# Early output of an MoE: gathers that add, one VectorE step in each expert's pause, other tiles and another order at the end

## The chip, the core and the metric

The kernel runs on one core of one Trainium2 chip. The metric is the device time of one execution in microseconds, lower is better. TensorE multiplies matrices, VectorE and ScalarE work on rows, GpSimd here issues the indirect DMAs and works on single columns, and SyncE issues the plain DMAs. Times in this text are microseconds (us), those inside a profile from the start of its span.

## The reference, cut to what matters

A trunk of two layers. Each ends with a mixture of experts, in which a token goes to 2 of 32 experts of one group; after the second layer every token's row is normalised and written out.

```python
def rmsnorm(x, g):
    xf = x.astype(jnp.float32)
    y = xf * lax.rsqrt(jnp.mean(xf * xf, axis=-1, keepdims=True) + RMS_EPS)
    return (y * g.astype(jnp.float32)).astype(x.dtype)
...
    def expert_block(args):
        e, xb = args
        return (jax.nn.silu(xb @ w_gate[e]) * (xb @ w_up[e])) @ w_down[e]
...
    for layer in range(DEPTH):
...
        h = h + hierarchical_moe(rmsnorm(h, ffn_norm[layer]), router_g[layer], router_g_bias[layer],
                                 router_e[layer], router_e_bias[layer], w_gate[layer], w_up[layer], w_down[layer])
...
    return rmsnorm(h, final_norm)[:, N_META:]
```

There are 1024 tokens and 16 rows of meta tokens that are dropped at the end; a row has 1024 float32 values, an expert's inner width is 256.

## The kernel before, in words

The change concerns the second layer's mixture, the last third of the program. `Moe.run` goes through 33 passes, e = 0 to 32. In pass e TensorE works on the gate and up products of expert e (96 rows at most) and on the down product of expert e−1. Float32 products are made from three pieces: ScalarE (L1552) and VectorE (L1553) split a weight tile `wp` in two roundings for a part of the products, the other part (`whole`, L953) runs in plain float32. SyncE loads weights (L898) into a ring of 17 slots of 1 MB; a load waits until VectorE has read the slot's old weights. GpSimd gathers an expert's rows (`ga`, L908) and scatters its results into the tensor `y_d` (L914), in which a token has two rows, one for each of its experts. VectorE writes an expert's results with its weights on them in L1002 (`rows`), once a pass.

In a pass VectorE's order is: down pieces, a pause in which it waits for ScalarE, up pieces, xq (L929), L1002, xT, hm (L978), and then the next pass's down pieces.

The class `Out` writes output while the loop still runs. On VectorE a chain of small steps (`order`: later, latest, masks, starts, places, suits) sorts the tokens by the later of their two experts. Eight indirect DMAs on GpSimd write the tokens' numbers to `list_d` (`place_ids`, L847), SyncE loads that list (`load_list`, L853), and VectorE makes row indices from it (`lists`, L858 to L862). The steps stand at the end of the pass (`end`), between hm and the next pass's pieces, except `sums`, which is at the pass's start.

The sorted tokens make seven tiles of 128. `EARLY_OUT` names for each tile the pass in whose beginning GpSimd gathers the tile's two rows of each token into two rooms (L1192). VectorE adds them (L1219) in the next pass, ScalarE squares and sums a row of 1024 (L1222), GpSimd makes the inverse root in 14 steps on single columns (`root`, L1228 to L1239 and L173), VectorE scales (L1242) and GpSimd stores by an indirect DMA (L1204). The tokens of the last three experts (`DIRECT`) are not in the tiles: their rows from these experts stay in SBUF, and only the other row is gathered (L1212). If a list does not suit (`bad`), the output is made again by `again` after the loop; that does not happen with these inputs.

The queues of the engines are in program order; a waiting instruction holds all that stands behind it on its engine. The order across engines is set by semaphores only.

## Time and profile before

| | us |
|---|---|
| median of three runs (1349.09 to 1350.46) | 1349.44 |
| profiled execution | 1349.53 |
| its span, first to last instruction | 1347.7 |
| TensorE busy in the span | 1267.6 (94%) |
| VectorE busy | 1055.0 (78%) |
| ScalarE busy | 748.0 (55%) |
| GpSimd busy | 401.9 (30%) |
| mean granted clock of TensorE | 0.971 |

The busy times are sums over the whole program, of which the part that is changed covers the stretch from about 1000 us to the end. What is limited by what has to be read from that stretch.

### The profile page before, as it was taken

How to read it: one execution, taken by the hardware profiler on the slowest of the kernel's cores; microseconds unless marked ns; L12 is line 12 of the kernel's file. 1: busy time of each engine (PE TensorE's matmuls, PEld its weight loads, DVE VectorE, ACT ScalarE, POOL GpSimd, SP SyncE). 2: the span in 40 equal slices, each digit the busy share in tenths (PEclk: the TensorE clock that was granted, in tenths of full speed). 3: DMA queues.
4: the chain of work that ended last, by engine and by line, in shares of the span. 5: the costliest groups of instructions: out<-in, count | busy, mean ns of one | idle time of the engine just before them, and what ended most of it. 6: DMA issues, size and time to landing. Idle time of an engine off the chain costs nothing. (4 is left out here: it accounts for less than half of the span.)

```text
span 1347.7 us, 22878 instructions
## 1 busy us (share of the span) xinstructions
PE 1267.6 (94%) x8029; PEld 1091.1 (81%) x8029; DVE 1055.0 (78%) x2490; ACT 748.0 (55%) x1595; POOL 401.9 (30%) x587
## 2 busy tenths in 40 slices
PE   7988999999999799999999999999699999999992
PEld 5977888888887799888998888999677778877771
DVE  5777888888888786667778677768879888888885
ACT  3435555555555555666655566555455566556552
POOL 0112122122220252022231222221312444545466
PEclk8998999999999899999999999999789999999996
DMA  8936999999980700304200010046779999999942
GB/s 306 409 125 203 369 363 370 349 352 358 358 304 30 267 25 1 120 1 170 93 25 16 9 36 17 17 161 224 279 259 293 340 389 377 366 369 357 342 175 77
DMA packets 81710, 293.12 MB, mean 217 GB/s; under 512 B 22897, under 2 KB 30321, under 8 KB 65075
## 3 DMA queue, kind: packets, MB, share of 16 engines
q1 hardware_dynamic: 63202, 245.54, 50.5%
q0 software_dynamic: 18384, 46.04, 9.9%
q8 instruction: 65, 1.06, 0.3%
q14 instruction: 59, 0.48, 0.1%
HBM read 270.75 MB, written 47.00 MB: 236 GB/s over the span
## 5 line engine op out<-in xcount | busy, mean ns | idle before, releaser
L1557 PE MATMUL gu<-wp,xT 128*96 128x256 f32 x512 | 147.3, 288 | 0.0
L1559 PE MATMUL gu<-wp,xT 128*96 128x256 f32 x512 | 143.4, 280 | 0.0
L1558 PE MATMUL gu<-wp,xT 128*96 128x256 f32 x512 | 143.3, 280 | 0.0
L1553 DVE TENSOR_TENSOR wp<-slotB,wp 128x512 fp32r<-128x512 f32 x160 | 107.0, 690 | 22.5 <-ACT wp L1552 21.6
L1557 PE MATMUL py<-wp,hT 128*96 128x512 f32 x256 | 112.7, 440 | 5.2 <-ACT hT L1552 5.2
L1552 ACT ACTIVATE wp<-slotB 128x512 fp32r<-128x512 f32 x160 | 96.0, 626 | 23.8 <-PE py L1559 20.2
L2460 POOL TENSOR_TENSOR hh<-hh,wt 128x512 f32<-128x512 f32 x56 | 72.4, 1293 | 111.4 <-ACT wt L2459 109.9
L1559 PE MATMUL py<-wp,hT 128*96 128x512 f32 x256 | 102.9, 402 | 2.1 <-DVE hT L1553 2.0
L914 POOL DMA_INDIRECT y_d<-xg,di x34 | 38.9, 1144 | 212.2 <-DVE xg L1002 205.7
L1558 PE MATMUL py<-wp,hT 128*96 128x512 f32 x256 | 101.5, 396 | 0.7 <-DVE wp L1553 0.7
L1552 ACT ACTIVATE xT<-xq 128x384 fp32r<-128x384 f32 x64 | 33.6, 526 | 111.1 <-DVE xq L929 107.9
L1557 PEld LDWEIGHTS gu<-wp,xT 128*96 128x96 f32 x512 | 84.8, 166 | 0.1
L1559 PEld LDWEIGHTS gu<-wp,xT 128*96 128x96 f32 x512 | 83.2, 162 | 0.0
L1558 PEld LDWEIGHTS gu<-wp,xT 128*96 128x96 f32 x512 | 82.9, 162 | 0.1
L953 PE MATMUL gu<-slotB,xq 128*96 128x256 f32 x320 | 75.6, 379 | 0.0
L2296 ACT ACTIVATE P<-bank,sm 128x400 f32<-128x400 f32 (+3 forms) x112 | 59.5, 539 | 25.8 <-DVE sm L2286 25.5
L2049 DVE TENSOR_TENSOR T<-bank,T 128x512 fp32r<-128x512 f32 (+2 forms) x112 | 53.7, 496 | 20.7 <-ACT T L2045 19.8
L929 DVE TENSOR_TENSOR xq<-pt,ffg 128x768 f32<-128x768 f32 (+1 forms) x66 | 61.0, 927 | 9.4 <-PE pt L926 9.4
L2463 DVE SCALAR_TENSOR_TENSOR hh<-bank,ri,hh 128x512 f32<-128x512 f32 x72 | 53.5, 747 | 16.8 <-PE bank L1559 16.4
L977 ACT ACTIVATE hm<-gu,table 96x256 f32<-96x256 f32 x64 | 30.0, 469 | 61.4 <-PE gu L1559 61.4
L1553 DVE TENSOR_TENSOR wp<-hh,wp 128x512 fp32r<-128x512 f32 x82 | 54.8, 689 | 11.8 <-ACT wp L1552 11.4
L2459 ACT ACTIVATE wt<-bank,ri 128x512 f32<-128x512 f32 x56 | 38.5, 688 | 41.7 <-PE bank L1559 34.6
(445 smaller groups left out, 4020.4 us busy)
## 6 DMA issues: line engine op xcount, KB each, us to landing
slotB<-w_up SPq DMA_DIRECT2D x20, 1024.0 KB
slotB<-w_down SPq DMA_DIRECT2D x20, 1024.0 KB
slotB<-w_gate SPq DMA_DIRECT2D x20, 1024.0 KB
hh<-w_gate SPq DMA_DIRECT2D x11, 1024.0 KB
hh<-w_up SPq DMA_DIRECT2D x10, 1024.0 KB
hh<-w_down SPq DMA_DIRECT2D x10, 1024.0 KB
slotR<-w_gate SPq DMA_DIRECT2D x10, 1024.0 KB
slotR<-w_up SPq DMA_DIRECT2D x10, 1024.0 KB
```

The costliest lines, as they stand in the source:

```text
L914: return nc.gpsimd.indirect_dma_start(out=self.r.y_d, out_offset=bass.IndirectOffsetOnAxis(ap=didx, axis=0), in_=y[:CAP], in_offset=None, ...
L929: nc.vector.tensor_tensor(x[:, 4 * a:4 * (a + w)].rearrange("p (a b) c -> p a b c", a=w), pt[:, a:a + w].rearrange("p a (b c) -> p a b c", ...
L953: nc.tensor.matmul(gu[:CAP, f * FE:f * FE + FE], lhsT=x[0][:, j], rhs=w[:, j], start=(f == 0 and j == 0), stop=False)
L1552: nc.scalar.activation(dH, src, AF.Copy)
L1553: nc.vector.tensor_tensor(dL, src, dH.bitcast(F32), op=OP.subtract)
L1557: nc.tensor.matmul(out, lhsT=aH, rhs=bH, start=start, stop=False)
L1558: nc.tensor.matmul(out, lhsT=aH, rhs=bL, start=False, stop=False)
L1559: nc.tensor.matmul(out, lhsT=aL, rhs=bH, start=False, stop=stop)
L2049: nc.vector.tensor_tensor(dL, src, dH.bitcast(F32), op=OP.subtract)
L2296: nc.scalar.activation(self.P[hd, qp][a][:, x0:x0 + xe], tt[:, :xe], AF.Exp, bias=sm[:, 3:4], scale=SCALE, accum_out=sm[:, x:x + 1])
L2460: done(end), s.op("G", end + s.LAT, 1170, lambda: nc.gpsimd.tensor_tensor(k.h[i][:, cs], k.h[i][:, cs], x, op=OP.add), lambda end: s.relea ...
L2463: s.op("V", now + s.LAT, 70 + 1.04 * 512, lambda: nc.vector.scalar_tensor_tensor(k.h[i][:, cs], p, self.ri[hd, i], k.h[i][:, cs], op0=OP.m ...
```

## The change

`EARLY_OUT` goes from (10, 14, 18, 22, 26, 30, 30) to (13, 17, 20, 24, 26, 29, 30). A tile's two gathers stand in two passes, and the second one adds to the first one's rows in the DMA (`compute_op`), so the VectorE addition of tiles is gone. ScalarE squares a tile in two halves into PSUM, and `root` has one step more, which adds the two sums. A tile goes through six passes: gather in pass f, adding gather in f+1, squares in f+2 (after the up pieces on ScalarE), root in f+3, scale in f+4, store in f+5; two rooms hold two tiles at a time. `end` and `middle` are replaced by `gap`, which puts at most a few VectorE instructions into the pause of a pass: the order's steps, cut into ten parts, in passes 1 to 15, and the scales. `place_ids` moves from pass 6 to 10, `load_list` from 8 to 11, `lists` from the end of pass 9 to the pause of pass 12. At the end tiles 5 and 6 use buffers of experts 27 and 26; the rows for the last three experts' tokens are gathered as before, one of them adding, and their roots, scales and stores come in another order.

```diff
-EARLY_OUT = (10, 14, 18, 22, 26, 30, 30)
+EARLY_OUT = (13, 17, 20, 24, 26, 29, 30)
...
-        return later, latest, masks, sums, starts, places, suits
+        return sums, {1: later, 2: latest, 3: masks, 4: numbers, 6: lambda: starts(0), 7: lambda: starts(3), 8: prefix, 9: places,
+                      11: suits, 12: self.lists, 15: self.tokens}
...
                 ps = self.down(hs, wd)
                 load(1)
+                if out:
+                    out.gap(e)
             if this and prev:
                 wp = self.up_pieces(e)
+                if out:
+                    out.squares(e)
...
-                    out.middle(e)
...
-            if out:
-                out.end(e)
+            if out and e == 0:
+                out.gap(0)
...
+    def fetch(self, x, rows, add=False):
+
+        n = rows.shape[0]
+        g = self.k.nc.gpsimd.indirect_dma_start(
+            out=x[:n], out_offset=None, in_=self.r.y_d, in_offset=bass.IndirectOffsetOnAxis(ap=rows, axis=0),
+            bounds_check=2 * L - 1, oob_is_err=False, compute_op=OP.add if add else OP.bypass)
+        self.got.append(g)
+        return g
...
+    def other(self, i, add=False):
+        self.fetch(self.sum[i], self.r.ti[:CAP, 1, i:i + 1], add)
...
+    def square(self, c, i, n=128):
         for j in range(2):
...
-        self.k.nc.scalar.activation(c[-1].bitcast(BF16)[:n, :D], c[0][:n], AF.Square, accum_out=self.st[:n, 0, i:i + 1])
+            self.k.nc.scalar.activation(self.junk[:n], c[:n, 512 * j:512 * j + 512], AF.Square,
+                                        accum_out=self.st[:n, 3 * j, i:i + 1])
 
...
+        eng.tensor_tensor(ss, ss, t, op=OP.add)
...
-        if e == 4:
-            sums()
+        if e == 0:
+            nc.vector.memset(self.st, 1.0)
+            nc.sync.dma_start(out=self.g, in_=bcast_row(k.A["final_norm"], D))
         if e == 6:
+            self.sums()
+        if e == 10:
             ids = []
             for i in range(len(r.tiles)):
                 x = r.place_ids(i)
                 self.apart(x, ids)
                 ids.append(x)
-        if e == 8:
+        if e == 11:
             r.load_list()
-        if 8 <= e < 8 + DIRECT:
-            r.load_tokens(e - 8)
-        for t, f in enumerate(EARLY_OUT[:-2]):
-            if e == f:
-                self.fetch(t, self.a)
+        if 12 <= e < 12 + DIRECT:
+            r.load_tokens(e - 12)
+        for t, f in enumerate(EARLY_OUT):
+            for j in range(2):
+                if e == f + j:
+                    x = self.fetch(self.rows[t], r.list[:, j, t:t + 1], j > 0)
+                    if t < len(EARLY_OUT) - 2:
+                        self.apart(x, [self.scat])
+            if e == f + 3 and t < 5:
+                self.root(t % 2)
+            if e == f + 5 and t < 5:
+                self.store_tile(t)
+        if e == NE - 1:
+            self.other(0, True)
+            self.other(1)
+            self.root(2)
+        if e == NE:
+            self.other(2)
+
+    def gap(self, e):
+
+        if e in self.order:
+            self.order[e]()
+        for t, f in enumerate(EARLY_OUT[:5]):
+            if e == f + 4:
+                self.scale(self.rows[t], t % 2)
+
+        if e == NE:
+            self.square(self.sum[0], 4, CAP)
+            self.root(3, n=2)
+
+    def squares(self, e):
+
+        for t, f in enumerate(EARLY_OUT[:5]):
             if e == f + 2:
-                self.root(0)
-            if e == f + 3:
-                self.store(t, self.a)
+                self.square(self.rows[t], t % 2)
         if e == NE - 2:
-            self.fetch(5, self.a)
-            self.fetch(6, self.b)
-            self.other(0, self.rows(0)[0])
+            self.square(self.rows[5], 2)
         if e == NE - 1:
-            self.root(0)
-            self.other(1, self.rows(1)[0])
-        if e == NE:
-            self.root(1)
-            self.other(2, self.rows(2)[0])
-            self.store(5, self.a)
-            self.root(2)
...
-        V = self.k.nc.vector
-        for f in EARLY_OUT[:-1]:
-            if e == f + 1 and f < NE - 2 or e == f == NE - 2:
-                self.add(V, self.a)
-            if e == f + 2 and f < NE - 2 or e - 1 == f == NE - 2:
-                self.scale(self.a, 0)
-        if e == NE - 1:
-            self.square(self.b, 1)
-
...
-        for x, f in ((0, later), (1, latest), (2, masks), (4, starts), (5, places), (7, suits), (9, r.lists), (11, r.tokens)):
-            if e == x:
-                f()
-        for f in EARLY_OUT[:-1]:
-            if e == f + 1 and f < NE - 2 or e == f == NE - 2:
-                self.square(self.a, 0)
-        if e == NE - 2:
-            self.add(V, self.b)
-        if e == NE - 1:
-            self.add(V, self.rows(0), CAP)
-            self.square(self.rows(0), 2, CAP)
...
+            self.square(self.rows[6], 3)
...
-        self.scale(self.b, 1)
+        self.scale(self.rows[5], 2)
+        self.store_tile(5)
...
-        self.scale(d[0], 2, CAP)
-        self.store(6, self.b)
+        for i in (1, 2):
+            self.add(self.sum[i], self.own[i], CAP)
+            self.square(self.sum[i], 4 + i, CAP)
+        self.scale(self.rows[6], 3)
         scatter()
-        self.root(3, V, 2)
-        self.scale(d[2], 4, CAP)
-        self.scale(d[1], 3, CAP)
-        for i in (0, 2, 1):
-            self.keep(d[i], r.ti[:CAP, 0, i:i + 1])
+        self.store_tile(6)
+        self.root(5, V, 2)
+        for i in (2, 0, 1):
+            self.scale(self.sum[i], 4 + i, CAP)
+            self.store(self.sum[i], r.ti[:CAP, 0, i:i + 1])
```

On VectorE, the place where the list's indices are made (`ids`, `list`; `wp` are weight pieces, `hm` and `hT` the expert's inner rows). Before:

```order
L978 SCALAR_TENSOR_TENSOR hm<-gu,table_5152,hm 96x256 [waits Activation_49]
L858 SCALAR_TENSOR_TENSOR ids<-past,ids 128x7 [waits DMASW5_49,DMASW6_49,DMASW4_49,DMASW7_49,DMASW3_49,DMAHW3_49,DMASW1_49,DMASW0_49]
L860 TENSOR_SCALAR ids<-ids 128x7 [waits DVE_49]
L862 TENSOR_SCALAR list<-ids 128x8 [waits DVE_49]
L862 TENSOR_SCALAR list<-ids 128x8
L1553 TENSOR_TENSOR wp_13239<-hh_11250,wp_13238 128x512 [waits DMAHW0_49,Activation_49]
L1553 TENSOR_TENSOR wp_13243<-hh_11250,wp_13242 128x512 [waits Activation_49]
L1553 TENSOR_TENSOR hT_13252<-ph,hT_13251 128x192 [waits Activation_49]
```

After, where the first two rows are the last down pieces of the pass and the wp rows behind L870 the up pieces:

```order
L1548 TENSOR_TENSOR wp_13469<-slotR_10855,wp_13468 128x512 [waits Activation_49]
L1548 TENSOR_TENSOR wp_13473<-slotR_10855,wp_13472 128x512 [waits Activation_49]
L866 SCALAR_TENSOR_TENSOR ids<-past,ids 128x7 [waits DMASW5_49,DMASW6_49,DMASW4_49,DMASW7_49,DMASW3_49,DMAHW4_49,DMASW1_49,DMASW0_49]
L868 TENSOR_SCALAR ids<-ids 128x7 [waits DVE_49]
L870 TENSOR_SCALAR list<-ids 128x8 [waits DVE_49]
L870 TENSOR_SCALAR list<-ids 128x8
L1548 TENSOR_TENSOR wp_13499<-slotR_10856,wp_13498 128x512 [waits DMAHW7_49,Activation_49]
L1548 TENSOR_TENSOR wp_13503<-slotR_10856,wp_13502 128x512 [waits Activation_49]
```

The same four instructions with the same wait for DMAs stand in another part of a pass, and three passes later.

On SyncE, the load of the list between weight loads. Before and after:

```order
L898 DMA qr<-w_gate 128x2048 [waits DMAHW2_49,DVE_49]
L853 DMA ids<-list_d 128x8x1 [waits DMASW5_49,DMASW4_49,DMASW6_49,DMASW3_49,DMASW7_49,DMASW2_49,DMAHW3_49,DMASW1_49,DMASW0_49]
L898 DMA qr<-w_up 128x2048 [waits DMAHW4_49,DVE_49]
```

```order
L906 DMA slot_11440<-w_gate 128x2048 [waits DMAHW3_49,DVE_49]
L861 DMA ids<-list_d 128x8x1 [waits DMASW5_49,DMASW4_49,DMASW6_49,DMASW3_49,DMASW7_49,DMASW2_49,DMAHW4_49,DMASW1_49,DMASW0_49]
L906 DMA slot_11441<-w_up 128x2048 [waits DMAHW5_49,DVE_49]
```

The load waits for all eight scatters; it has moved nine weight loads, three passes, down the queue.

On GpSimd, the last gathers of tiles (`list`) and of the last experts' tokens (`ti`), from the pass before the last two. Before:

```order
L1192 DMA out_11729<-y_d_5148,list 128x1024 [waits DMASW3_49,DMASW1_49]
L1192 DMA out_11730<-y_d_5148,list 128x1024
L1192 DMA xg_11723<-y_d_5148,list 128x1024 [waits DMASW5_49,DMASW6_49,DMASW2_49,PE_49]
L1192 DMA xgh<-y_d_5148,list 128x1024 [waits DMASW0_49,PE_49]
L1212 DMA hh_11725<-y_d_5148,ti 96x1024 [waits DMASW7_49,PE_49]
L914 DMA y_d_5148<-hh_11725,di_5154 2080x1024 [waits DVE_49]
L1228 TENSOR_SCALAR ost<-ost 128x1 [waits Activation_49]
L173 TENSOR_SCALAR ost<-ost 128x1 [waits Pool_49]
```

After:

```order
L1206 DMA xgh<-y_d_5148,list 128x1024 [waits DMASW7_49,PE_49]
L922 DMA y_d_5148<-hh_11725,di_5154 2080x1024 [waits DVE_49]
L1206 DMA xgh<-y_d_5148,list 128x1024 [waits DMASW3_49,DMASW2_49,DMASW1_49]
L1206 DMA xg_11723<-y_d_5148,list 128x1024 [waits DMASW5_49,DMASW4_49]
L922 DMA y_d_5148<-hh_11725,di_5154 2080x1024 [waits DVE_49]
L1214 DMA out<-out_11729,list 1024x1024 [waits DMASW6_49]
L1206 DMA xg_11723<-y_d_5148,list 128x1024 [waits DMASW5_49,DMASW4_49]
L1206 DMA hh_11725<-y_d_5148,ti 96x1024 [waits DMASW0_49,PE_49]
L1206 DMA hh_11725<-y_d_5148,ti 96x1024
```

Of the four gathers of tiles 5 and 6 that stood together, the second ones now wait for DMAs before them, and two gathers for the last experts stand in one group ahead of the root.

## Rows read from the trace of the kernel before

**Rows 1.** Busy time by stretch: us, then each engine, TensorE clock, DMA share, GB/s

```profile
1041.00:1065.00 24.00, 21.17 (x127) 16.63 (x126) 19.25 (x37) 11.73 (x22) 12.35 (x12) 1.00 0.99 336
...
1230.00:1272.00 42.00, 41.61 (x253) 33.66 (x252) 36.79 (x55) 24.77 (x46) 20.08 (x25) 1.00 1.00 360
...
1304.00:1326.00 22.00, 16.61 (x78) 11.48 (x76) 17.49 (x24) 11.65 (x23) 16.54 (x32) 0.86 0.20 63
```

**Rows 2.** VectorE timeline: start us, duration, line, output and inputs, idle before

```profile
999.67 1.27 DVE L1002 SCALAR_TENSOR_TENSOR xg<-py,table,xg 96x1024 f32<-96x1024 f32 x1
...
1052.55 1.27 DVE L1002 SCALAR_TENSOR_TENSOR hh<-py,table,hh 96x1024 f32<-96x1024 f32 x1
...
1065.11 1.27 DVE L1002 SCALAR_TENSOR_TENSOR xg<-py,table,xg 96x1024 f32<-96x1024 f32 x1
...
1075.23 1.27 DVE L1002 SCALAR_TENSOR_TENSOR xg<-py,table,xg 96x1024 f32<-96x1024 f32 x1
...
1085.32 1.27 DVE L1002 SCALAR_TENSOR_TENSOR xg<-py,table,xg 96x1024 f32<-96x1024 f32 x1
...
1087.37 0.48 DVE L978 SCALAR_TENSOR_TENSOR hm<-gu,table,hm 96x256 f32<-96x256 f32 x1 [0.32 <-issue]
1087.77 0.15 DVE L858 SCALAR_TENSOR_TENSOR ids<-past,ids 128x7 f32<-128x7 f32 x1
...
1101.94 1.37 DVE L1553 TENSOR_TENSOR wp<-slot,wp 128x512 fp32r<-128x512 f32 x2 [0.91 <-ACT wp L1552]
...
1105.50 1.27 DVE L1002 SCALAR_TENSOR_TENSOR hh<-py,table,hh 96x1024 f32<-96x1024 f32 x1
...
1303.61 1.27 DVE L1002 SCALAR_TENSOR_TENSOR hh<-py,table,hh 96x1024 f32<-96x1024 f32 x1
```

**Rows 3.** Costs by line on VectorE, 1000 to 1348 us: busy us, mean ns, idle before

```profile
L1242 DVE SCALAR_TENSOR_TENSOR out<-out,ost,out 128x1024 f32<-128x1024 f32 (+1 forms) x7 | 8.9, 1274 | 0.0
```

**Rows 4.** TensorE timeline: the first half of the next expert after the pause of 1101.94

```profile
1103.96 0.34 PE L1557 MATMUL gu<-wp,xT 128*96 128x256 f32 x1
```

**Rows 5.** ScalarE timeline after expert 5's rows: the wait for TensorE

```profile
1059.54 0.33 ACT L1552 ACTIVATE hT<-ph 128x192 fp32r<-128x192 f32 x1 [2.79 <-PE gu L953]
```

**Rows 6.** GpSimd timeline around the list's scatters

```profile
1046.57 1.24 POOL L847 DMA_INDIRECT list_d<-ids,place  x1 [1.57 <-DVE place L826]
...
1056.20 0.97 POOL L847 DMA_INDIRECT list_d<-ids,place  x1 [0.30 <-issue]
...
1089.44 1.05 POOL L869 DMA_INDIRECT token<-later_d,gi  x1 [0.30 <-issue]
```

**Rows 7.** SyncE's queue: the list's load and the next load

```profile
1064.99 0.38 SPq L853 DMA_DIRECT2D ids<-list_d  x1
1071.65 4.52 SPq L898 DMA_DIRECT2D qr<-w_up  x1
```

**Rows 8.** GpSimd timeline from the last gathers of tiles to the last store

```profile
1301.02 1.27 POOL L1192 DMA_INDIRECT xgh<-y_d,list  x1 [0.30 <-issue]
...
1307.80 0.19 POOL L1228 TENSOR_SCALAR ost<-ost 128x1 f32<-128x1 f32 x1 [0.49 <-ACT out L1222]
...
1315.28 0.19 POOL L1239 TENSOR_TENSOR ost<-ost 128x1 f32<-128x1 f32 x1
...
1325.17 1.58 POOL L1212 DMA_INDIRECT xgh<-y_d,ti  x1 [0.67 <-issue]
...
1340.65 0.91 POOL L1204 DMA_INDIRECT out<-out,ti  x1 [0.30 <-issue]
```

**Rows 9.** VectorE timeline of the same stretch: the additions that waited for gathers

```profile
1307.88 1.23 DVE L1219 TENSOR_TENSOR xg<-xg,xgh 128x1024 f32<-128x1024 f32 x1 [1.01 <-DMA xgh<-y_d,list]
...
1329.88 1.22 DVE L1219 TENSOR_TENSOR xgh<-xgh,xg 96x1024 f32<-96x1024 f32 x1 [0.94 <-DMA xgh<-y_d,ti]
```

**Rows 10.** GpSimd timeline: a tile's store and the gather that waits for it

```profile
1247.19 1.14 POOL L1204 DMA_INDIRECT out<-out,list  x1 [0.30 <-DVE wp L1553]
...
1259.61 1.08 POOL L1192 DMA_INDIRECT out<-y_d,list  x1 [3.60 <-DMA out<-out,list]
```

More of the change, by code (lines that the diff above doesn't have):

```diff
@@ L808, in sums, with starts @@
             k.nc.tensor.matmul(pr[:, 1], lhsT=k.ones, rhs=self.cnt, start=True, stop=True)
-        def starts():
-            a = tot
-            V.tensor_copy(tot, pr[:, 1])
-            for i, n2 in enumerate((1, 2, 4, 8, 16)):
+        def starts(i):
+            a = cum[(i - 1) % 2] if i else tot
+            if i == 0:
+                V.tensor_copy(tot, pr[:, 1])
+            for i, n2 in ((0, 1), (1, 2), (2, 4)) if i == 0 else ((3, 8), (4, 16)):
                 x = cum[i % 2]
@@ L1177, in __init__ @@
     def __init__(self, k, r, psum, out, room, g):
-        self.k, self.r, self.out, self.g = k, r, out, g
-        self.a, self.b = room, [k.xg[(NE - 6) % NX], k.xg[(NE - 5) % NX]]
-        self.st = k.route.tile([128, 4, 5], F32, name="ost")
+        self.k, self.r, self.out, self.g, self.a = k, r, out, g, room
+        x = [k.xg[e % NX] for e in range(NE)]
+        self.rows = [room[t % 2] for t in range(5)] + [x[NE - 5], x[NE - 6]]
+        self.own = x[NE - DIRECT:]
+        self.sum = [self.own[0], x[NE - 4], room[1]]
+        self.junk = psum.tile([128, 512], F32, name="junk", tag="junk", bufs=1)
+        self.st = k.route.tile([128, 4, 7], F32, name="ost")
         self.got, self.put = [], []
-        self.order = r.order(psum, room)
+        self.sums, self.order = r.order(self.junk, room)
     def apart(self, x, others):
@@ new lines, in store, with store_tile @@
+    def store(self, x, ids):
+        n = ids.shape[0]
+        p = self.k.nc.gpsimd.indirect_dma_start(
+            out=self.out[0], out_offset=bass.IndirectOffsetOnAxis(ap=ids, axis=0), in_=x[:n], in_offset=None,
+            bounds_check=S - 1, oob_is_err=False)
+        self.apart(p, self.put)
+        self.put.append(p)
+    def store_tile(self, t):
+        self.store(self.rows[t], self.r.list[:, 0, t:t + 1])
+    def other(self, i, add=False):
+        self.fetch(self.sum[i], self.r.ti[:CAP, 1, i:i + 1], add)
@@ L1241, in scale @@
     def scale(self, c, i, n=128):
-        self.k.nc.vector.scalar_tensor_tensor(c[0][:n], c[0][:n], self.st[:n, 2, i:i + 1], self.g[:n], op0=OP.mult, op1=OP.mult)
-    def rows(self, i):
-        x = self.k.xg
-        free = x[(NE - DIRECT) % NX]
-        return [(x[(NE - 4) % NX], self.a[1], self.b[1])[i], x[(NE - DIRECT + i) % NX], self.b[1] if i == 0 else free]
+        self.k.nc.vector.scalar_tensor_tensor(c[:n], c[:n], self.st[:n, 2, i:i + 1], self.g[:n], op0=OP.mult, op1=OP.mult)
     def begin(self, e):
         k, r, nc = self.k, self.r, self.k.nc
-        later, latest, masks, sums, starts, places, suits = self.order
-        if e == 4:
-            sums()
+        if e == 0:
+            nc.vector.memset(self.st, 1.0)
+            nc.sync.dma_start(out=self.g, in_=bcast_row(k.A["final_norm"], D))
         if e == 6:
+            self.sums()
+        if e == 10:
             ids = []
@@ L1343, in again @@
                     m.fetch(t, j, c[j])
-                self.add(nc.vector, c)
-                self.square(c, 0)
+                self.add(*c)
+                self.square(c[0], 0)
                 self.root(0, nc.vector)
-                self.scale(c, 0)
+                self.scale(c[0], 0)
                 nc.sync.dma_start(out=self.out[0, t * 128:(t + 1) * 128], in_=c[0])
```

52 lines of the change are left out of this document (10 added, 42 removed).

## The prediction

> **What bounds the kernel now.** I read the table of stretches first, then VectorE's timeline for the distance from one expert's rows (L1002) to the next, and last the queues of the three engines that issue DMAs. From 1041 us on, the loop of the second MoE keeps the 16 DMA engines busy all the time and TensorE and VectorE nearly so; after 1304 the DMA share falls to 0.20 and TensorE is busy in three quarters of the time [rows 1]. So there are two bounds: the loop's period, and after 1304 GpSimd's queue of gathers, roots and stores.
>
> I write A(e) for the start of L1002 in pass e, which stores expert e−1. An undisturbed period is 10.09 us, from 1075.23 to 1085.32 [rows 2]. Five periods from 999.67 to 1052.55 take 52.88, which is 2.43 over five such periods: the order steps at the end of passes 0 to 5. The next period takes 12.56, 2.47 over. The 22 periods from 1075.23 to 1303.61 take 228.38, 6.4 over: each of five tiles has an addition and a scale of 1.27 there [rows 3], and about half of the two shows. Those 11.3 us are all that the early output costs inside the loop.
>
> **What the change takes away.** In its pause before the up pieces VectorE waits 0.91 us for ScalarE, with 3.56 us to go to L1002 [rows 2]. A scale of 1.27 put there overshoots by 0.4, and the steps of the order, cut into more parts, by less than 0.7. Two rows take that up: VectorE idles 0.32 before hm at 1087.37 [rows 2], and TensorE starts the next expert's halves at 1103.96, 1.3 after the first up piece is made [rows 4]. So I cost these steps at nothing; without that cover the five scales would cost 2 us. The additions go to the gathers. That gives −2.4 for the order and −6.4 for the tiles. The long period after 1052.55 is unclear: ScalarE waited 2.79 us for TensorE at 1059.54 while GpSimd issued the eight scatters of the list [rows 5, 6]. These scatters return four passes later. The bounds are 0 and −2.5, nothing in the rows tells which, and I take −1.2.
>
> **What it adds in the loop.** *The list.* Eight scatters write it, SyncE loads it, and VectorE makes the indices. Before, the scatters ran from 1046.57 to 1056.20 (start of the last), the load was issued at 1064.99, and VectorE used it at 1087.77 with no wait shown: 22.8 us after the load's issue [rows 2, 6, 7]. Now the scatters stand in pass 10, the load at the start of pass 11 and the use in the pause of pass 12. GpSimd comes to the scatters where the small gather at 1089.44 stands, 4.1 after A [rows 2, 6], so the last starts at A(9)+4.1+9.6 = A(10)+3.6. It lands no later than 8.8 after its start (1056.20 to 1064.99, the load waits for it) [rows 6, 7]. I take 8, so the load leaves at A(11)+1.5. The use stands before the up pieces due 3.56 before A(12), that is at A(11)+6.5. How long the load takes no row shows. Below it is bounded by 6.9, the gather of 1301.02 awaited at 1307.88 when the DMA was nearly idle [rows 8, 9]; above by the 22.8. The nearest row is SyncE's own next load, which was issued at 1071.65 and held its queue for 4.52, to 1076.17: 11.2 after the list's load [rows 7]. I take 11.2. The indices are then there at A(11)+12.7, 6.2 late, plus 0.6 for the three steps, less 1.1 of slack (between the 0.32 and the 1.3 above, nearer the latter as TensorE sets the pace): **+5.7**. Behind the waiting step on VectorE stand the four up pieces, xq and L1002, so TensorE and ScalarE wait too. The bounds are +1.4 and +17. For its stand-still afterwards I add 1.0: between 1304 and 1326, with TensorE idle a quarter of the time, its granted clock was 0.86 of full speed on average [rows 1], so part of that stretch ran at the half level, 1.2 GHz.
>
> The Trainium skill, in "DMA: Bandwidth & Descriptors", section "Rules for kernel authors", says that a DMA with a non-contiguous last dimension becomes one descriptor an element; for this load that is 1024. By its section "Bandwidth" 64 packets an engine take about 0.67 us, and its section "Anatomy of one DMA" puts a fixed 2.0 us beside that: an estimate of 2.7, with no wait at all and a time about 6.7 us lower. That is the page's case for an idle DMA; the trace here has a share of 1.00, and the held queue of 4.52 us [rows 7] speaks against it.
>
> *The gathers.* A tile's second gather now adds to the first's rows, so it waits until these have landed, and ScalarE's squares come a pass later. While the DMA is full a transfer lands up to 12.4 us after its issue (the store of 1247.19, for which the gather of 1259.61 waited 3.60) [rows 10]; in the idle stretch it was 6.9. I take 10. For the first, second and fourth tile that leaves 1 to 4 us to spare. For the third (gathers in passes 20 and 21) and fifth (26 and 27), a root of up to 7.7 us stands on GpSimd ahead of the first or second gather [rows 8]. The rows then land about 2 us after they are due in ScalarE's queue, whose next work is xT: **+2 each**, bounds 0 and 3.3. Whether an adding gather moves more bytes no row shows; at 360 GB/s [rows 1] one more read of 0.5 MB would be 1.4 us a tile on engines whose share has fallen to 0.20 by 1304, so nothing.
>
> **The end.** Set 0 at 1303.61 (A(30)). Now the last store is issued at 1340.65, 37.0 after it, and the span ends 7.05 later, at 44.1 [rows 2, 8]. After, GpSimd has in this order: the first gather of tile 6 (done at 1.3), the scatter of expert 29 (2.8), a store (4.1), the adding gather, which waits for that scatter to land (4.7 as from 1325.17 to 1329.88 [rows 8, 9]; done 8.4), two gathers for the last experts (11.4), a root of 15 steps for tile 5 (12.9 to 19.4; the 14 steps of before took 7.7 [rows 8], other ones 5.1 to 5.5), the scatter of expert 30 (20.4), its landing and the last gather (26.7), a root for two columns at once (32.0). VectorE then scales tile 6 (33.4), makes its own root (35.8) and three scales; the last store is issued at 39.8 and the span ends at 46.8: **+2.7**. Tile 5's squares wait for a gather that leaves only in their own pass, so TensorE stands some 5.5 us in pass 30; that makes its last rows come at 27, still ahead of GpSimd's 32.0, and costs nothing more. Removing one root and one store at the end is paid for by three waits for landings in a row.
>
> **The sum.** 1347.7 − 2.4 − 6.4 − 1.2 + 5.7 + 1.0 + 2 + 2 + 2.7 = 1351.1. The profiled execution took 1349.53, 1.83 more than its span and 0.09 more than the median of 1349.44. So: **1352.9 us**, 0.26% above the median. About 0.2% (2.7 us) is what a measurement here tells from no change.
>
> **The rivals.**
> *The list lands in time.* Then 6.7 us fall away: 1346.2. It decides if the load lands within 6 us of its issue; for it speaks that the use had no wait before, against it that this use was 22.8 us behind, and now is 5. Chance 0.30. The Trainium skill's estimate above is this case.
> *The DMA sets the loop's pace.* Its share is 0.99 to 1.00 from 1041 to 1272 [rows 1]. If weights were late, a shorter loop would only wait for them: the 10.0 us of gain are lost, the list's stall costs nothing as the loads catch up, and the tail's 2.7 stays: 1352.2. Against it: the pause of 1101.94 ended with ScalarE, not with a load [rows 2], and after 1304 the share is 0.20. Chance 0.10.
> *The steps don't fit the pauses.* The scales and the order's steps push every up piece back, so that half of the 8.8 us is not gained, and the eight scatters stall TensorE as before: 1352.9 + 4.4 + 1.2 = 1358.5. Chance 0.15.
> *The forecast*: the list is late by 3 to 10 us. Chance 0.45.
>
> The bounds together: the list at +1.4 without a drop of the clock, gathers in time and the scatters harmless give 1342.3; the list at +10 and the late gathers at 3.3 each give 1360. I take **1343 to 1360**; the list at +17 lies outside. Faster by over 0.2% (under 1346.7): 0.29, nearly all from the first rival. Within 0.2%: 0.26, from the low part of the forecast and the second rival. Slower: 0.45.
>
> **What would show it.** In pass 12 VectorE's first index step should wait some 6 us on a DMA, with TensorE idle behind it; the periods of passes 1 to 6 and of tiles 1, 2 and 4 should be 10.1; ScalarE's squares of tiles 3 and 5 should wait for gathers; the last third should be GpSimd's chain, its last store about 40 us after expert 29's rows. The prediction is wrong if the list step shows no wait, or if GpSimd's chain ends before TensorE's last rows.

## The result

| | before | after |
|---|---|---|
| median of ten runs each | 1349.27 | 1356.07 |
| lowest to highest | 1347.88 to 1352.24 | 1353.15 to 1361.27 |
| profiled execution | 1349.53 | 1353.48 |
| its span | 1347.7 | 1351.7 |
| mean granted clock of TensorE | 0.971 | 0.963 |

The ratio is 1.0051, with an interval of 1.0034 to 1.0068: slower by half a per cent, 6.8 us where 3.5 were forecast. The profiled execution is one of the lower ones of after; its rows explain 4.0 us, and what makes up the other 2.6 of the median no row shows.

The table of stretches of after, which answers to [rows 1]:

```profile
1105.00:1147.00 42.00, 35.97 (x204) 29.69 (x203) 29.65 (x53) 20.42 (x38) 15.49 (x13) 0.92 0.99 348
...
1230.00:1272.00 42.00, 41.49 (x253) 34.20 (x252) 35.60 (x54) 25.82 (x50) 20.24 (x27) 1.00 1.00 349
...
1304.00:1326.00 22.00, 16.11 (x92) 12.55 (x90) 13.27 (x21) 11.84 (x27) 14.04 (x23) 0.92 0.53 124
1326.00:1351.70 25.70, 2.66 (x11) 1.54 (x10) 12.99 (x23) 4.59 (x13) 13.59 (x23) 0.61 0.29 94
```

A stretch with 6 us of idle TensorE has appeared at 1105. From 1230 to 1272 the DMA is as full as before and moves 349 GB/s instead of 360. From 1304 to 1326 its share is 0.53 instead of 0.20; the adding gathers of tiles 5 and 6 run there now, issued at 1303.59 and 1313.87, where before issued its last gather of a tile at 1301.02 [rows 8].

VectorE's timeline of after: the rows of an expert (L1010, which was L1002), and the first index step of the list. It answers to [rows 2]:

```profile
997.76 1.27 DVE L1010 SCALAR_TENSOR_TENSOR xg<-py,table,xg 96x1024 f32<-96x1024 f32 x1
...
1048.35 1.27 DVE L1010 SCALAR_TENSOR_TENSOR hh<-py,table,hh 96x1024 f32<-96x1024 f32 x1
...
1088.70 1.27 DVE L1010 SCALAR_TENSOR_TENSOR xgh<-py,table,xgh 96x1024 f32<-96x1024 f32 x1
1101.97 1.27 DVE L1010 SCALAR_TENSOR_TENSOR hh<-py,table,hh 96x1024 f32<-96x1024 f32 x1
...
1114.76 0.17 DVE L866 SCALAR_TENSOR_TENSOR ids<-past,ids 128x7 f32<-128x7 f32 x1 [7.97 <-DMA ids<-list_d]
...
1118.59 1.27 DVE L1010 SCALAR_TENSOR_TENSOR hh<-py,table,hh 96x1024 f32<-96x1024 f32 x1
1129.25 1.27 DVE L1010 SCALAR_TENSOR_TENSOR xg<-py,table,xg 96x1024 f32<-96x1024 f32 x1
...
1220.06 1.27 DVE L1010 SCALAR_TENSOR_TENSOR xgh<-py,table,xgh 96x1024 f32<-96x1024 f32 x1
1234.22 1.27 DVE L1010 SCALAR_TENSOR_TENSOR hh<-py,table,hh 96x1024 f32<-96x1024 f32 x1
...
1306.47 1.27 DVE L1010 SCALAR_TENSOR_TENSOR hh<-py,table,hh 96x1024 f32<-96x1024 f32 x1
1321.99 1.27 DVE L1010 SCALAR_TENSOR_TENSOR xg<-py,table,xg 96x1024 f32<-96x1024 f32 x1
```

The first five periods take 50.59 us, 10.12 each: the order's steps are hidden. Four periods are over 12 us: 13.27 to 1101.97, 16.62 to 1118.59, 14.16 to 1234.22, and 15.52 to 1321.99. In all A(1) to A(30) takes 308.71 us, 16.1 over 29 periods of 10.09, where before took 303.94, 11.3 over. A(1) itself stands 1.9 earlier than in [rows 2]; over the profiles of this study it lies between 994.9 and 999.7, so lengths from A(1) on are what can be compared. From A(1) to the end after takes 5.9 us more than before, not 4.0. The wait of 7.97 for the list explains the second; TensorE stands behind it:

```profile
1116.06 0.53 PE L1553 MATMUL gu<-wp,xT 128*96 128x256 f32 x1 [6.03 <-DVE wp L1548]
```

ScalarE's timeline of after has the waits in the other three:

```profile
1095.02 0.33 ACT L1547 ACTIVATE hT<-ph 128x192 fp32r<-128x192 f32 x1 [2.86 <-PE gu L961]
...
1222.47 0.60 ACT L1231 ACTIVATE junk<-out 128x512 f32<-128x512 f32 x1 [3.92 <-DMA out<-y_d,list]
...
1311.16 0.60 ACT L1231 ACTIVATE junk<-xgh 128x512 f32<-128x512 f32 x1 [6.20 <-DMA xgh<-y_d,list]
```

The first is the wait of [rows 5] again, now in the pass to which the eight list scatters have moved. The second is the third tile (gathers in passes 20 and 21), the third is tile 5 counted from 0 (gathers in passes 29 and 30). Here "the third tile" counts from 1 and "tile 5" from 0, as in the prediction. The issuers' queues of after, GpSimd's first, then SyncE's; they answer to [rows 6 to 8, 10]:

```profile
1092.90 0.97 POOL L855 DMA_INDIRECT list_d<-ids,place  x1 [0.30 <-issue]
...
1103.52 2.60 POOL L922 DMA_INDIRECT y_d<-hh,di  x1 [7.12 <-DMA y_d<-xgh,di]
...
1201.05 1.13 POOL L1206 DMA_INDIRECT out<-y_d,list  x1 [0.52 <-issue]
...
1210.51 1.62 POOL L1206 DMA_INDIRECT out<-y_d,list  x1 [5.75 <-DMA out<-y_d,list]
...
1303.59 1.69 POOL L1206 DMA_INDIRECT xgh<-y_d,list  x1 [4.07 <-issue]
...
1313.87 1.60 POOL L1206 DMA_INDIRECT xg<-y_d,list  x1 [3.60 <-DMA y_d<-hh,di]
...
1329.46 1.01 POOL L1206 DMA_INDIRECT out<-y_d,ti  x1 [2.70 <-DMA y_d<-xg,di]
...
1344.65 0.91 POOL L1214 DMA_INDIRECT out<-hh,ti  x1 [0.30 <-issue]
```

```profile
1100.43 0.38 SPq L861 DMA_DIRECT2D ids<-list_d  x1
1100.90 5.23 SPq L906 DMA_DIRECT2D slot<-w_up  x1
```

The list's load is used 14.3 us after its issue and holds SyncE's next load for 5.23. The third tile's adding gather leaves at 1210.51, because GpSimd waited for the first gather, and has landed at 1222.47, 12.0 later. The last store is issued at 1344.65, 38.2 after A(30).

The queues' page of after, and the same row of before (packets, MB, share of 16 engines' span):

```profile
q0 software_dynamic: 18384, 46.04, 10.8%
...
HBM read 270.75 MB, written 47.00 MB: 235 GB/s over the span
```

```profile
q0 software_dynamic: 18384, 46.04, 9.9%
```

GpSimd's transfers have the same packets and bytes and take more of the engines' time: 0.108 of 1351.7 is 146.0 us of all 16, against 133.4. The share is printed to 0.1%, so each of these is good to some 0.7 us.

### The profile page after: what moved, and what is told of

It reads as the page before. It is cut to its first block, busy times and chain, and to the rows that moved or that the text cites. A ratio compares the mean times of both kernels' runs of the same rounds, so it can differ in the third digit from the quotient of the medians.

```text
span 1351.7 us, 22865 instructions
## 1 busy us (share of the span) xinstructions
PE 1267.8 (94%) x8029; PEld 1100.0 (81%) x8029; DVE 1045.9 (77%) x2483; ACT 749.7 (55%) x1615; POOL 391.0 (29%) x580
## 3 DMA queue, kind: packets, MB, share of 16 engines
q1 hardware_dynamic: 63202, 245.54, 50.4%
q0 software_dynamic: 18384, 46.04, 10.8%
## 5 line engine op out<-in xcount | busy, mean ns | idle before, releaser
L922 POOL DMA_INDIRECT y_d<-xg,di x34 | 34.2, 1006 | 202.6 <-DVE xg L1010 194.9
L2276 DVE TENSOR_REDUCE mx<-bank 128x1 f32<-128x400 f32 (+3 forms) x112 | 55.5, 505 | 7.6 <-PE bank L2262 5.6
```

What stands on the lines that cost most here:

```text
L2276: V.tensor_reduce(m[:, ci:ci + 1], t[:, :e], axis=AX.X, op=OP.max)
```

## Experiments

Theory 1 at the start: the list's late load is what costs. Rivals: the time lost there would be lost elsewhere, as the DMA or GpSimd's queue is the bound; or the adding gathers cost DMA time, which the prediction had at nothing. A(e) is as before, now with L1010. Each kernel is compared with runs of before on the same chip.

**1. The list a pass later** (before's median 1348.02 there, also for 2 to 4)

```diff
-EARLY_OUT = (13, 17, 20, 24, 26, 29, 30)
+EARLY_OUT = (14, 17, 20, 24, 26, 29, 30)
...
-                      11: suits, 12: self.lists, 15: self.tokens}
+                      11: suits, 13: self.lists, 15: self.tokens}
```

> The changed kernel with the list's index steps in the pause of pass 13 in place of 12, and the first tile gathered in pass 14 in place of 13. My theory: the list lands about 14 us after its load is issued, so a use ten microseconds later finds it there; VectorE's wait of 8.0 us on the list vanishes, the period of 16.62 becomes 10.1, and the time falls by 6 to 7 us, to about 1349.5. Rival: the list step only shows a backlog of the DMA that some later transfer would show anyway (weights late, first tile late), so the wait turns up elsewhere and the time falls by less than 2 us.

Measured: 1354.48, ratio 1.0047 (1.0022 to 1.0071), not told apart from after's 1.0051: a fall of under 2 us, as the rival had it. In the profiled execution the use still waited:

```profile
1121.01 0.17 DVE L866 SCALAR_TENSOR_TENSOR ids<-past,ids 128x7 f32<-128x7 f32 x1 [4.65 <-DMA ids<-list_d]
```

The load, issued at 1103.06, was used 18.0 us later, so a pass more of room did not cover it in this execution: the load took 3.7 us longer than in after, and the stall behind the list's scatters, which in after held the use back by 3.2 us as well, did not come. What was won was not kept: period 30 (to A(31)) was 19.24 instead of 15.52.

**2. Gathers ahead of roots**: in addition, GpSimd issues a pass's gathers ahead of its root.

```diff
         for t, f in enumerate(EARLY_OUT):
             for j in range(2):
...
+        for t, f in enumerate(EARLY_OUT):
             if e == f + 3 and t < 5:
                 self.root(t % 2)
```

> As the run before, and in each pass's beginning GpSimd issues the gathers of tiles ahead of the roots. Theory: the third tile's rows were late because a root of 7 us stood ahead of its first gather; now the gather leaves 7 us earlier, ScalarE's wait of 3.9 us for them and the long period of 14.16 vanish, that of 10.83 for the fifth tile too: 4 to 5 us less than the run before. Rival: the adding gather itself is slow (a transfer that reads its destination), and the rows are late by 2 us or more in any order.

Measured: 1355.89, one run, so 4 to 5 us less did not show. It speaks most against theory 1. The list was in time, the third tile's period was 10.09, the scatters did not stall, and the rows of expert 24 stood at 1241.07, 10.8 us ahead of before's 1251.88 (0.8 of it at A(1)). None of it was left at the end (span 1354.1). TensorE's timeline:

```profile
1255.39 1.94 PE L961 MATMUL gu<-hh,xq 128*96 128x256 f32 x8 [1.46 <-DMA hh<-w_gate]
...
1259.38 1.97 PE L961 MATMUL gu<-slot,xq 128*96 128x256 f32 x8 [1.88 <-DMA slot<-w_up]
...
1271.52 1.97 PE L961 MATMUL gu<-slotR,xq 128*96 128x256 f32 x8 [1.53 <-DMA slotR<-w_up]
...
1284.26 2.97 PE L961 MATMUL gu<-slotR,xq 128*96 128x256 f32 x8 [2.41 <-DMA slotR<-w_up]
```

TensorE waits for weights, for which it waits nowhere from 1235 to 1300 in before and after. The periods to A(26) to A(29) are 11.35, 13.88, 12.15 and 14.39: 11.4 us over. Then ScalarE waits 10.98 for tile 5, and the period to A(31) is 20.50. The loop without the list's wait runs into the DMA here. The table of stretches of this kernel has the rate:

```profile
1225.00:1250.00 25.00, 24.00 (x141) 19.46 (x140) 20.72 (x32) 14.28 (x27) 10.40 (x9) 1.00 1.00 336
1250.00:1275.00 25.00, 20.05 (x122) 16.20 (x121) 17.59 (x27) 12.22 (x26) 11.69 (x21) 1.00 0.99 344
```

**3. Tile 5's squares and root a pass later**, on top of 2:

```diff
         if e == NE - 1:
             self.other(0, True)
             self.other(1)
-            self.root(2)
...
+        if e == NE - 1:
+            self.square(self.rows[5], 2)
+            self.root(2)
...
-        if e == NE - 2:
-            self.square(self.rows[5], 2)
```

> As the run before, and the squares of tile 5 stand on ScalarE in the pause of pass 31 in place of pass 30, with the root for them behind them. Theory: TensorE's stall of 5.4 us in pass 30 vanishes (period of 15.52 to about 10.5), but the end is set by GpSimd's chain of gathers, roots and scatters, so the end moves by less than 1.5 us. Rival: TensorE's last rows set the end, and the time falls by the whole stall, 4 to 5 us.

Measured: 1359.59, ratio 1.0089 (1.007 to 1.0108): slower than after, which neither expectation had. The stall of pass 30 went into two, with periods of 13.98 and 13.91; ScalarE's timeline:

```profile
1313.42 0.60 ACT L1231 ACTIVATE junk<-xgh 128x512 f32<-128x512 f32 x1 [4.73 <-DMA xgh<-y_d,list]
...
1324.07 0.60 ACT L1231 ACTIVATE junk<-xg 128x512 f32<-128x512 f32 x1 [7.10 <-DMA xg<-y_d,list]
```

**4. The list loaded twice**: after, with a second load of the same shape ahead of the real one.

```diff
         if e == 11:
+            with nc.allow_non_contiguous_dma("one number a row"):
+                nc.sync.dma_start(out=self.twice, in_=r.list_d.rearrange("(t p) o -> p (t o)", p=128))
             r.load_list()
```

> The changed kernel with a second load of the same list, into a tile that nobody reads, ahead of the first on SyncE's queue. Theory: the list's 1024 single elements take their time one after another, so a second such load ahead of it makes VectorE's wait on the list longer by 6 to 12 us (from 8.0 to 14 to 20). Rival: the wait is the latency behind the queued weights, which a small load more does not change: the wait stays at 7 to 10 us.

Measured: 1355.52. VectorE waited 4.8 us longer than in after, and SyncE's queue was held by the real load too:

```profile
1114.33 0.17 DVE L866 SCALAR_TENSOR_TENSOR ids<-past,ids 128x7 f32<-128x7 f32 x1 [12.78 <-DMA ids<-list_d]
```

```profile
1099.56 8.39 SPq L861 DMA_DIRECT2D ids<-list_d  x1
1108.05 5.07 SPq L906 DMA_DIRECT2D slot<-w_up  x1
```

One such load costs some 5 to 8 us on this queue. The increase of 4.8 lies between the two expectations, nearer the theory's. The one run's 1355.52 lies among after's, but A(1) came 2.8 us earlier and the scatters did not stall, which gave 3.1 back; from A(1) to the end this profile is 4.8 us longer than after's, so in this execution the longer wait did reach the end. The trace also shows what such a load is made of: the hardware queue has 64242 packets instead of 63202, 1040 more for the second load of 1024 numbers.

**5 and 6. Plain second gathers**: the second gather overwrites instead of adding, in experiment 2's kernel and in after itself (before's median 1349.33, also for 7 and 8).

```diff
-            bounds_check=2 * L - 1, oob_is_err=False, compute_op=OP.add if add else OP.bypass)
+            bounds_check=2 * L - 1, oob_is_err=False, compute_op=OP.bypass)
```

> The kernel of gathers_ahead_of_roots, with every adding gather as a plain one to the same place: as many gathers, bytes and waits, but the second row replaces the first, so the sum of the two rows is left out. In gathers_ahead_of_roots the loop was 10.8 us ahead of the kernel before by expert 24, and lost it when TensorE waited for up and gate weights in passes 25 to 28, with the DMA engines full at 335 to 344 GB/s against 360 before. Theory: the adding gathers make the DMA engines read the destination too, 0.5 MB a tile and some 10 us in all, and this makes the weights late. Then the rate at a full share goes back to about 360, the last weights land 7 to 10 us earlier, the waits for weights go, and the time falls by 6 us or more, below that of the kernel before (about 1343). Rival: the weights are late because the loop runs ahead of the DMA, whatever the gathers do: the waits stay and the time changes by less than 2 us.

> The changed kernel itself, with every adding gather as a plain one to the same place (the sum of the two rows is left out). The first theory: about 4 to 6 us less than the changed kernel, since the third tile's rows come earlier and the last weights too, but the wait of 8 us on the list stays, so about 1350. Rival: nothing, as in the changed kernel the loop is not ahead of the weights.

Measured: 1352.27 for experiment 2's kernel, ratio 1.0019 (1.0004 to 1.0033), where it was 1355.89; and **1349.58 for after**, ratio 0.9996 (0.9976 to 1.0015), where it was 1356.07. The intervals of after with and without the adding (1.0034 to 1.0068) do not meet: the adding in the DMA costs about 6.5 us by the medians, nearly all of the loss (before's medians beside them are 1349.33 and 1349.27). That is as the theory had it for after; in experiment 2's kernel the fall is 3.6 us against one run, not the 6 or more that the theory had. VectorE's timeline of after with plain gathers, and its queue row:

```profile
1119.50 0.17 DVE L866 SCALAR_TENSOR_TENSOR ids<-past,ids 128x7 f32<-128x7 f32 x1 [9.51 <-DMA ids<-list_d]
...
1225.66 1.27 DVE L1010 SCALAR_TENSOR_TENSOR xgh<-py,table,xgh 96x1024 f32<-96x1024 f32 x1
1236.50 1.27 DVE L1010 SCALAR_TENSOR_TENSOR hh<-py,table,hh 96x1024 f32<-96x1024 f32 x1
...
1307.96 1.27 DVE L1010 SCALAR_TENSOR_TENSOR hh<-py,table,hh 96x1024 f32<-96x1024 f32 x1
1321.36 1.27 DVE L1010 SCALAR_TENSOR_TENSOR xg<-py,table,xg 96x1024 f32<-96x1024 f32 x1
```

```profile
q0 software_dynamic: 18384, 46.04, 10.2%
```

The list's wait is even longer (9.51). The third tile's period fell from 14.16 to 10.84 and that of pass 30 from 15.52 to 13.40, 5.4 us together, and these are the places where a gather is waited for. The two profiled executions differ by only 1.1 us, since this one is the third longest of its ten: A(1) stands 2.0 later in it and the list's two periods are 3.7 longer, and all the rest is 6.7 shorter. GpSimd's transfers take 0.102 of 1350.6 us, 8.2 less than in after; over the study the queue's share is 10.7% to 11.0% in the six profiles with adding gathers and 9.9% to 10.2% in the eight without. From 1304 to 1326 both move 124 GB/s, at a DMA share of 0.39 here and 0.53 in after. In experiment 2's kernel the waits for weights are gone; from 1250 to 1275 the DMA moves 361 GB/s instead of 344:

```profile
1250.00:1275.00 25.00, 24.30 (x150) 20.07 (x149) 20.10 (x31) 15.73 (x30) 10.92 (x21) 1.00 0.99 361
```

What it gains is lost again at the end: GpSimd's first gather for tile 5 waited 8.32 for a scatter to land (1289.25), the root behind it came late for VectorE's scale (a wait of 4.44, period 14.54), and ScalarE waited 12.16 for tile 5's second gather:

```profile
1306.77 0.60 ACT L1231 ACTIVATE junk<-xgh 128x512 f32<-128x512 f32 x1 [12.16 <-DMA xgh<-y_d,list]
```

**7. The order's steps in the pauses alone**: before with this one part, the scatters in pass 8, the load in pass 9, the indices and the first tile's gathers in the pause of pass 11.

```diff
-EARLY_OUT = (10, 14, 18, 22, 26, 30, 30)
+EARLY_OUT = (11, 14, 18, 22, 26, 30, 30)
...
+                if out:
+                    out.gap(e)
...
-        if e == 6:
+        if e == 8:
...
-        if e == 8:
+        if e == 9:
             r.load_list()
...
+    def gap(self, e):
+        if e in self.order:
+            self.order[e]()
+        if e == EARLY_OUT[0]:
+            self.fetch(0, self.a)
```

> The kernel before with only the order's steps moved into VectorE's pauses (passes 1 to 13); tiles, roots and the end as before. The scatters of the list stand in pass 8, its load at the start of pass 9, the index steps in the pause of pass 11, and the first tile's gathers right behind them; the other tiles stand where they did. Theory: 2.4 us of order steps go, nothing is added, the weights have enough lead for that: a period of 10.1 in passes 1 to 6 and 1346 to 1347. Rival: the loop already runs at the DMA's pace, and what it gains early is lost to weights before the end: no change within 1 us.

Measured: 1355.55, ratio 1.0044 (1.0031 to 1.0058), more than either expectation. The part itself did what it should: A(1) to A(8) took 70.82 instead of 75.56; 2.5 of this is the scatters' stall, which came a period later here (14.00), and 2.3 the order's steps. But I had left three passes between the first two tiles, which share their rooms, and GpSimd's gather waited for the first tile's store:

```profile
1141.46 1.02 POOL L1202 DMA_INDIRECT out<-y_d,list  x1 [10.72 <-DMA out<-out,list]
```

VectorE's addition then waited 7.49, and that period was 20.72. The experiment shows what a tight schedule costs while the DMA is full, and does not price the part.

**8. Before again**, one more profile of the old kernel:

> The kernel before, once more. ScalarE's wait of 2.8 us for TensorE while the eight scatters are issued (period of 12.56) was there in the changed kernel (13.28), but not in the three kernels run since with the same scatters (10.16). Theory: it is an event that comes in some executions and not in others, and has no fixed place: this run may show it elsewhere or not at all. Rival: it belongs to the scatters in pass 6 and comes again, at 2 to 3 us.

Measured: 1352.91. The period that holds the eight scatters, 12.56 in [rows 2], was 15.00 here, and ScalarE waited longer:

```profile
1060.34 0.33 ACT L1552 ACTIVATE hT<-ph 128x192 fp32r<-128x192 f32 x1 [3.56 <-remote]
```

In the profiles of this study the pass of the scatters took 12.6 to 15.0 in six (the two of before, after, 5, 6 and 7) and 10.0 to 10.2 in seven (1 to 4, 9, 11 and 12), among these 12, in which nothing around the scatters differs from before. The stall has moved with the scatters, to passes 10 (after, 5, 6) and 8 (7), so it belongs to them, and it is not there every time; what decides it stays open. It goes by sets of runs: all four of 5 to 8, which ran on one chip at one time, had it, and none of 1 to 4, of 9 and 10 or of 11 and 12.

**9. Pauses without adding gathers**: before with the order's steps and the additions in the pauses, a tile's two plain gathers a pass apart, in two rooms a tile (before's median 1348.67, also for 10).

```diff
-            if e == f:
-                self.fetch(t, self.a)
-            if e == f + 2:
-                self.root(0)
+            if e == f and t:
+                self.fetch(t, self.pair(t), (0,))
+            if e == f + 1:
+                self.fetch(t, self.pair(t), (1,))
+            if e == f + 3:
+                self.root(0)
...
+    def gap(self, e):
+        if e in self.order:
+            self.order[e]()
...
+            if e == f + 2:
+                self.add(self.k.nc.vector, self.pair(t))
```

> A version built from the kernel before: the order's steps in VectorE's pauses, and the tiles with two plain gathers a pass apart, where the next tile's first rows go to the room that the last tile's addition has freed; the addition (1.21 us) in the pause two passes after the first gather, squares behind the up pieces, root a pass later, the scale where the kernel before has it (0.4 us shows), the store at the end of that pass. Tiles 5 and 6 as in the kernel before, in the other order. Theory: what costs the change its gain is the read that the adding gathers add to full DMA engines, the wait for the list and the chain at the end; without all three about 1.5 us of order steps and 4.5 of tiles stay gained, the weights' lead is enough, and the time is 1343 to 1345. Rival: any lead of the loop over the DMA is lost again to late weights: 1348 to 1350.

Measured: 1360.74, ratio 1.0089 (1.0067 to 1.0111), far above both expectations. VectorE's additions waited for the second gather, issued a pass earlier; the waits from 1100 to 1320, with their sum, number and longest:

```profile
DVE out L1232 <- DMA out<-y_d,list: 17.7, 4, 6.2
```

A pass is too short for a gather here, and on VectorE everything stands behind the addition. So a version without adding gathers and without late rows has not been measured.

**10. The list's scatters in two halves**: before, with four in pass 6 and four in pass 7.

```diff
-        if e == 6:
-            ids = []
-            for i in range(len(r.tiles)):
+        if e in (6, 7):
+            ids = self.ids = self.ids if e == 7 else []
+            n = len(r.tiles)
+            for i in range(n // 2 * (e - 6), n // 2 * (e - 5)):
```

> The kernel before with four of the list's eight scatters in pass 6 and four in pass 7. In six of ten profiles so far the period behind the eight scatters was 2.5 to 5 us long, in four it was not. Theory: eight scatters hold GpSimd's queue and the DMA for 10 us; four of them do no harm, and both periods are 10.1 to 10.5. Rival: the event has nothing to do with their number: a period of 12 us or more in one of the two passes.

Measured: 1348.75, one run. Both periods were 10.1; as 9, run beside it with all eight scatters in one pass, had no stall either, this does not tell whether four scatters do less harm than eight. A(30) stood 3.1 us earlier than in [rows 2], at 1300.49. The next period gave it back, 13.92 instead of 10.89, as VectorE waited for tile 5:

```profile
1306.22 1.23 DVE L1219 TENSOR_TENSOR xg<-xg,xgh 128x1024 f32<-128x1024 f32 x1 [2.48 <-DMA xgh<-y_d,list]
```

**11 and 12. Fewer weights**: the loads of the down weights of experts 20 to 31 are left out, 12 MB, in experiment 2's kernel and in before (before's median 1349.35).

```diff
+        if self.out and e >= 20 and m == 2:
+            return
```

> The kernel of gathers_ahead_of_roots (the change with the list a pass later and the gathers ahead of the roots, adding gathers as they are) without the loads of the down weights of experts 20 to 31, 12 MB or some 33 us of full DMA engines; the products then use what the slots held before, so the output of these experts is left out. Theory: with room on the DMA engines the weights are no longer late, the loop keeps the 10.8 us by which it was ahead of the kernel before at expert 24, and the gathers at the end land in 5 to 7 us: 1344 to 1347, 9 to 12 us less than with all weights (1355.9). Rival: the end is GpSimd's own chain, whatever the DMA does: 1352 or more.

> The kernel before, without the same loads (the output of experts 20 to 31 is left out as well). Theory: its loop does not wait for weights and its gathers hardly for room, so it gains 1 to 3 us: 1346 to 1348. Rival: it too is bound by the DMA at the end, and gains 5 us or more.

Measured: 1350.83, ratio 1.0019 (1.0001 to 1.0036), for experiment 2's kernel, 5 us less than that kernel's one run with all weights and nearer to the rival's 1352 than to the theory's 1344 to 1347; and 1349.59, ratio 0.9994 (0.9978 to 1.001), for before, which gains nothing. So before loses no time to its weights, and experiment 2's kernel does. With fewer weights its periods from A(24) to A(30) are all 10.1 and the DMA share from 1275 to 1300 is 0.30, and still ScalarE waits for tile 5; ScalarE's row, and GpSimd's issue of that gather:

```profile
1302.57 0.60 ACT L1233 ACTIVATE junk<-xgh 128x512 f32<-128x512 f32 x1 [7.75 <-DMA xgh<-y_d,list]
```

```profile
1296.22 1.63 POOL L1208 DMA_INDIRECT xgh<-y_d,list  x1 [3.45 <-issue]
```

The gather lands 6.4 us after its issue even here, and is issued too late. From A(1) to A(30) this loop is 3.9 us shorter than before's (300.04; 7.0 are lost in one period, at the third tile), and its tail from A(30) is 48.2 instead of 44.1: the late gather of tile 5 and the chain of GpSimd behind it give all of it back. This profile is the second shortest of its ten, 4.2 us below their median; against before's span its 3.2 us are the 3.4 by which A(1) came earlier. No kernel here beat before by more than the measurement tells.

## Why the prediction was right, and where it was not

The forecast, slower by some microseconds and inside the range, was right. The profiled execution even met the sum: 1351.7 for 1351.1. That is luck: the loop lost 4.1 us more than the terms say, the tail lost 1.6 less, and A(1), ahead of everything that the sum is about, came 1.9 earlier. And the loss in the medians has another cause than the sum names. The steps:

- **The order's steps, −2.4**: right. The first five periods are 0.1 over five times 10.09, where 2.43 had been. So the third rival, that the steps don't fit the pauses, fell, though the stall at the scatters that it also had did come.
- **The tiles' additions and scales, −6.4**: right. The periods of the first and second tile are 10.1. That of the fourth, which was to be so too with 1 to 4 us to spare, is 10.83, as its squares waited 2.27 for the adding gather.
- **The list's scatters, −1.2**: wrong. The stall moved with the scatters and was 3.2 where before had 2.5, so +0.7. It belongs to the scatters (8) and comes in some executions.
- **The list, +5.7 and +1.0**: the mechanism was right, the size by luck. The step waited 7.97 with TensorE idle behind it, and its two periods are 7.1 over. But the load landed after 14.3 us instead of 11.2, and the lateness came out as forecast because the stall at the scatters put the use 3.2 later. The Trainium skill ("DMA: Bandwidth & Descriptors", "Rules for kernel authors") says that such a load becomes one descriptor an element; the trace agrees, with 1040 packets for one more load of 1024 numbers (4). The estimate of 2.7 us that I made from its sections "Bandwidth" and "Anatomy of one DMA", whose figures stand there for DMAs that GpSimd issues, did not hold for this load of SyncE on a full DMA (14.3), and so the rival by it fell.
- **Late gathers, +2 each**: the third tile cost 4.1, the fifth 0.9 and the fourth, which had none in the sum, 0.7. The third's adding gather took 12.0 where I had 10.
- **The tail, +2.7**: 45.2 us from A(30) to the end for 46.8, so 1.1 longer than before's. The order of GpSimd's chain was as forecast, down to the stand of TensorE in pass 30 (5.4 for 5.5).
- **"Whether an adding gather moves more bytes no row shows; ... so nothing"**: this is the step that failed. The sum made after slower by the list's wait, the late gathers and the tail, and had the adding at nothing; the runs showed that without the adding there is no loss, list's wait and all (6). My own price stood beside it, 1.4 us a tile, and I dropped it because the DMA share had fallen to 0.20 by 1304. But the gathers of the first four tiles run while the share is 1.00, and there every extra microsecond delays the gathers and weights behind it. Seven tiles of 1.4 are 9.8, and there is an eighth adding gather, of 96 rows; the runs showed 6.5 in time and 8.2 of engine time (6). The Trainium skill says, in the same section of that page, that an accumulating DMA reads its destination and writes it later. The traces fit that in time alone, as the counted bytes are the same; whether it is the read or the addition itself that takes the time, no run here shows.

The biggest surprise is not in the sum. I read the list's wait as the cost of the change, and as such it stands in the timeline. But a loop without it (2) ended no earlier, and with plain gathers it was no faster either (1352.27 without the wait, 1349.58 with it). The second rival, that the DMA sets the pace, had a chance of 0.10 since its share fell after 1304; but in the kernels with the list a pass later and adding gathers TensorE does wait for weights (2, 3 and, less, 1). With plain gathers these waits are gone (5), and before gains nothing from fewer weights (12), so it is the adding gathers that use up the slack that before had. So the loss of after is that of its adding gathers, and the list's wait hides the loop's gain: in each kernel that was run without that wait (2, 5, 11), the DMA or the end took the gain instead. That it would be so in any version is argued and not shown. How the end divides between DMA and GpSimd's chain is not settled; without weights in the way (11) tile 5's late gather and the chain behind it took back what the loop had won.

## What to carry to other kernels

An addition that a DMA does is not free when the DMA is full: price it as a transfer of its own (by its bytes that was too much here, 9.8 us and more for 6.5), and check the queue's share of time, since the bytes don't show it. When the loop that you shorten has other bounds close by, as this one had, price the gain at the distance to the next bound and not at the length of the wait that you remove. Between the issue and the use of a transfer leave what the trace shows at that place (here 9.5 to 18 us under a full DMA, 4.5 to 7.6 where its share was 0.2 to 0.6), not what it takes alone.

## What the runs showed of the hardware

- Adding gathers left the counted bytes at 46.04 MB and raised the queue's share from 10.2% to 10.8% (6 and after); the moved rate at a DMA share of 0.99 fell from 361 to 344 GB/s (2 and 5). From 1250 to 1275 it is 327 to 348 GB/s in the five profiles with adding gathers and a full DMA, and 359 to 372 in the seven with plain ones.
- A load of 1024 single numbers (4 KB) is 1040 packets (4). On a full DMA it was used 14.3 us after its issue and held the next load on SyncE for 5.23 (18.0 and 8.78 in 1); with a second one ahead, the holds were 8.39 and 5.07.
- The pass with eight indirect scatters of single numbers was 2.5 to 5 us longer than the others in six profiles and not in seven; it went by sets of runs and not by kernel, and its cause is open.
